# Storing the MLP's weight-block sums whole and splitting them where they are used

## The chip, the cores and the metric

The kernel runs on one core of a Trainium2 chip. A core has a matrix engine (PE, TensorE), a vector engine (DVE), a scalar engine (ACT), GpSimd (POOL) and a queue engine (SP) that here issues nearly all transfers (DMA). Matrix products write into PSUM, eight banks of 128 x 512 fp32; everything else lives in SBUF, 128 partitions wide. Each engine works off its own instruction stream in order and waits on semaphores for the others. The metric is device microseconds of one execution. The kernel before took 3085.63 us (median of 3 runs, 3080.34 to 3088.36).

## The reference, cut to what matters

One layer of a hybrid decoder runs on 2048 prompt tokens and 32 sample tokens (8 sequences of 4), all fp32, model width 1024:

```
h  = rmsnorm(x, g_mix);  proj = h @ w_in                 # 1024 x 4624
y  = [ RG-LRU mixer(proj) , Mamba-2 SSD mixer(proj) ]    # "the mixers"
x  = x + y @ w_out                                       # 2048 x 1024
m  = rmsnorm(x, g_mlp)
x  = x + square(relu(m @ w_up)) @ w_down                 # 1024 x 4096, 4096 x 1024
out = rmsnorm(x, g_final)
```

It also returns the states of both mixers. `w_up` and `w_down` are used by the MLP alone.

## The kernel before, in words

**Two-part products.** A matrix product of fp32 operands is made of three products of a reduced fp32 type (float32r). Each operand is split in a high part (ACT copies it to float32r) and a low part (DVE subtracts the high part from the original). The product adds high x high, high x low and low x high into one PSUM bank. `mm3` (lines 226 to 235) does so for the mixers, with weights split by `load_w` (an ACT copy in line 220, a DVE subtraction in line 222); `product` (lines 826 to 833) does it for the MLP.

**Mixers.** The 2080 tokens go through the mixers in three parts, each of two blocks of columns (384 and 384, 384 and 288, 384 and 256). In each part come the input projection and the SSD pairs (`pair_front`, `pair_x`, `pair_mats`, `pair_back`, eight times), then the LRU heads (`lru_front`, `lru_back`, eight times), then the output projection (`proj_add`, which multiplies and adds each PSUM bank on DVE, lines 445 and 446), then the transposes of the next part (`x_phase`).

**Weight blocks made in the mixers.** The MLP multiplies 2 x 2 blocks with seven products in place of eight (a Strassen-like scheme), so it needs seven combinations of each four weight blocks: four blocks and three sums. These don't depend on the tokens, and while the mixers run 64 jobs make them: 32 for `w_up`, 32 for `w_down`. A job has six stages: `job_load` issues eight DMAs of 64 KB into a tile `jt` of 128 x 7 x 256 (line 1128); `job_first` and `job_second` make the sums with four DVE additions of 128 x 256 (1133 to 1139); `job_higher` rounds all seven into a tile `jh` on ACT (1143); `job_lower` stores `jh` and starts to subtract, `job_store` subtracts the rest on DVE (1146) and stores the low parts (1150, 1155). `jt` and `jh` have one buffer each, so the next job's loads wait until both stores have landed. The mixers call `tick` at fixed places with a weight; each whole unit emits the next stage, 64 x 6 = 384 in all.

**MLP.** The tokens go through the MLP in three column blocks (2 x 348, 2 x 346, 2 x 346 columns). `front` loads the normalised tokens and makes the seven combinations of four k-blocks, each split in two. Then eight steps q follow: `up` twice (u = 0, 1), each seven products of 12 matmuls, with sums, relu, square and the seven combinations of the result (`operands`, `halves`) on ACT and DVE; then `down`, four groups g of seven products of 6 matmuls, each ended by a DVE addition out of PSUM (line 951). One weight load serves 12 matmuls: one product of `up`, or two of `down` (the seventh comes alone). The tile `mw` holds the high and the low parts and has six buffers; the DMA is issued by SP (lines 823 and 961). PSUM gives the products six banks, of which an `up` or a group of `down` takes four. In the last q of a column block the `front` of the next one is emitted among the groups of `down`, and the `final` norm of a block among the products of the next block's first two `up`s.

**What sets the order.** The framework orders each engine's instructions when the program is built: an instruction goes in when its inputs and buffers are planned to be there, earlier program text first. So the streams are not the program text; around the end of an `up`, PE takes the first halves of several `down` products before the second halves. Waits on the chip are fixed by that order.

## Time and profile before

| | before |
|---|---|
| median of 3 runs | 3085.63 us (3080.34 to 3088.36) |
| profiled execution | 3082.9 us, span 3081.2 us |
| PE busy | 2888.0 us (94%) |
| DVE busy | 2168.8 us (70%) |
| ACT busy | 1390.9 us (45%) |
| DMA | 708.99 MB, 230 GB/s; HBM read 541.43 MB, written 164.27 MB |
| mean granted TensorE clock | 0.970 |

The mixers take the time up to about 1700 us, the MLP the rest. A row of a windows view gives, for a stretch of the span, its length and then the busy microseconds of PE, PEld (the weight load of PE), DVE, ACT and POOL with the number of instructions, the granted TensorE clock, the DMA share and GB/s. A row of a group gives line, engine, operation, output <- input, shape and count, then busy time and mean duration, then the idle time of the engine before these and what ended it. A row of the chain of waits gives start, length and what the end of the program waited for at that time. A row of waits gives the waiting engine and line, what released it, the sum, the number of times and the longest.

### The profile page before, as it was taken

What the parts mean: (1) busy time and instruction counts of PE and PEld (TensorE: products, weight loads), DVE (VectorE), ACT (ScalarE), POOL (GpSimd) and SP (SyncE); (2) the same over time, 40 slices, a digit from 0 to 9 for tenths busy, and PEclk for the clock granted to TensorE, in tenths of its full rate; (3) what the DMA queues carried; (4) which work ended last, traced back from release to release, by engine and by line L of the source; (5) the groups of instructions that cost most, each with busy time, mean ns of one, the idle gap of its engine ahead of it and who ended that gap; (6) DMA issues with size and microseconds to landing.
All of it is one profiled execution on the core that took longest, in us unless ns stands there. A gap on an engine that the chain in (4) does not pass through costs nothing.

```text
span 3081.2 us, 49470 instructions
## 1 busy us (share of the span) xinstructions
PE 2888.0 (94%) x18150; PEld 2789.5 (91%) x18150; DVE 2168.8 (70%) x4422; ACT 1390.9 (45%) x2580; POOL 171.1 (6%) x270
## 2 busy tenths in 40 slices
PE   6999998989999898899989699999999999999997
PEld 6999897888988887899989599999999999999997
DVE  6888788688777878888787645556845556654556
ACT  5553685354357845444883323233432223432322
POOL 0000120010001300000120000000000000000000
PEclk9999998999999998999999799999999999999999
DMA  5555556766665577666656888888988888988885
GB/s 177 156 186 162 165 178 198 236 199 185 205 192 177 179 239 228 184 195 189 194 183 222 277 289 267 281 277 272 319 280 271 284 267 280 318 265 281 268 276 202
DMA packets 534481, 708.99 MB, mean 230 GB/s; under 512 B 44421, under 2 KB 414265, under 8 KB 534240
## 3 DMA queue, kind: packets, MB, share of 16 engines
q1 hardware_dynamic: 534016, 705.56, 71.8%
q8 instruction: 144, 2.36, 0.3%
q0 software_dynamic: 224, 0.27, 0.1%
q14 instruction: 97, 0.79, 0.1%
HBM read 541.43 MB, written 164.27 MB: 229 GB/s over the span
## 4 chain that ended last, share of the span: by engine, by line
PE 47%; DVE 8%; DMA 5%; ACT 4%; issue 1%; SPq 1%; POOL 0%; DVEq 0%; ACTq 0%
PE mb L832 39%; PE mm L235 2%; PE mm L233 2%; PE mm L234 2%; DVE jt L1146 1%; SPq L1128 1%; DMA dn<-jt 1%; DMA up<-jt 1%; DMA mb<-mn_d 1%; DMA mw<-dn 1%; DMA m<-cum 1%; DVE u L412 1%; DVE yt L1027 1%; DVE th L794 0%; ACT jh L1143 0%
## 5 line engine op out<-in xcount | busy, mean ns | idle before, releaser
L233 PE MATMUL mm<-xh,wh 128*128 128x384 f32 (+3 forms) x2160 | 712.6, 331 | 31.8 <-ACT xe L399 14.5
L235 PE MATMUL mm<-xh,wl 128*128 128x384 f32 (+3 forms) x2160 | 705.8, 328 | 3.9 <-DVE wl L222 3.8
L234 PE MATMUL mm<-xl,wh 128*128 128x384 f32 (+3 forms) x2160 | 705.4, 327 | 0.1
L832 PE MATMUL mb<-mhh,mw 128*128 128x346 f32 (+1 forms) x2688 | 655.2, 323 | 17.2 <-ACT mhh L839 16.6
L832 PE MATMUL mb<-ahh,mw 128*128 128x346 f32 (+1 forms) x2688 | 652.5, 323 | 13.1 <-DVE x L951 4.4
L832 PEld LDWEIGHTS mb<-mhh,mw 128*128 128x128 f32 x2688 | 475.8, 191 | 19.4 <-ACT mhh L839 18.3
L832 PEld LDWEIGHTS mb<-ahh,mw 128*128 128x128 f32 x2688 | 470.7, 189 | 19.6 <-ACT ahh L839 5.7
L233 PEld LDWEIGHTS mm<-xh,wh 128*128 128x128 f32 (+1 forms) x2160 | 409.0, 190 | 47.4 <-ACT xe L399 17.5
L832 PE MATMUL mb<-mhl,mw 128*128 128x346 f32 (+1 forms) x1344 | 437.3, 326 | 1.4 <-DVE mhl L840 1.4
L832 PE MATMUL mb<-ahl,mw 128*128 128x346 f32 (+1 forms) x1344 | 434.1, 323 | 0.4 <-DVE ahl L840 0.2
L235 PEld LDWEIGHTS mm<-xh,wl 128*128 128x128 f32 (+1 forms) x2160 | 408.2, 189 | 13.0 <-DVE wl L222 6.5
L234 PEld LDWEIGHTS mm<-xl,wh 128*128 128x128 f32 (+1 forms) x2160 | 409.0, 189 | 3.8 <-issue 1.0
L951 DVE TENSOR_TENSOR x<-x,mb 128x346 f32<-128x346 f32 (+1 forms) x480 | 244.5, 514 | 144.4 <-PE mb L832 143.1
L220 ACT ACTIVATE wh<-raw 128x1024 fp32r<-128x1024 f32 (+1 forms) x159 | 165.4, 1042 | 241.0 <-PE mm L234 181.0
L832 PEld LDWEIGHTS mb<-mhl,mw 128*128 128x128 f32 x1344 | 255.0, 190 | 2.8 <-DVE mhl L840 2.6
L832 PEld LDWEIGHTS mb<-ahl,mw 128*128 128x128 f32 x1344 | 253.7, 189 | 1.4 <-DVE ahl L840 1.4
L910 ACT ACTIVATE p<-mb 128x346 f32<-128x346 f32 (+1 forms) x48 | 21.9, 457 | 473.0 <-PE mb L832 470.9
L222 DVE TENSOR_TENSOR wl<-raw,wh 128x1024 fp32r<-128x1024 f32 (+1 forms) x159 | 190.7, 1201 | 20.5 <-ACT wh L220 19.4
L412 DVE SCALAR_TENSOR_TENSOR u<-xe,prm,u 128x768 f32<-128x768 f32 (+2 forms) x180 | 169.9, 944 | 16.6 <-ACT u L410 14.6
L233 PE MATMUL mm<-nh,wh 128*128 128x384 f32 (+2 forms) x384 | 131.2, 342 | 30.8 <-DVE x L446 27.8
L937 ACT ACTIVATE c<-c 128x346 f32<-128x346 f32 (+1 forms) x144 | 71.3, 495 | 192.5 <-DVE c L923 114.6
L1146 DVE TENSOR_TENSOR jt<-jt,jh 128x1024 fp32r<-128x1024 f32 (+1 forms) x128 | 137.9, 1094 | 25.0 <-ACT jh L1143 24.8
(305 smaller groups left out, 4218.6 us busy)
## 6 DMA issues: line engine op xcount, KB each, us to landing
mw<-up SPq DMA_DIRECT2D x336, 512.0 KB
mw<-dn SPq DMA_DIRECT2D x288, 512.0 KB
raw<-in_w_in_dram SPq DMA_DIRECT2D x108, 512.0 KB
up<-jh SPq DMA_DIRECT2D x32, 896.0 KB
up<-jt SPq DMA_DIRECT2D x32, 896.0 KB
dn<-jh SPq DMA_DIRECT2D x32, 896.0 KB
dn<-jt SPq DMA_DIRECT2D x32, 896.0 KB
raw<-in_w_out_dram SPq DMA_DIRECT2D x48, 512.0 KB
```

The source lines that it names most:

```text
L220: S.activation(h, raw, AF.Copy)
L222: V.tensor_tensor(out=lo, in0=raw, in1=h.bitcast(F32), op=ALU.subtract)
L233: T.matmul(ps[:m, :n], h[:, k, :m], xh[:, c0:c0 + n], start=k == 0, stop=False)
L234: T.matmul(ps[:m, :n], h[:, k, :m], xl[:, c0:c0 + n], start=False, stop=False)
L235: T.matmul(ps[:m, :n], lo[:, k, :m], xh[:, c0:c0 + n], start=False, stop=k == nk - 1)
L412: V.scalar_tensor_tensor(out=u[:, :W], in0=xe[:, k:k + W], scalar=pc(wn, k * nt + j), in1=u[:, :W], op0=ALU.mult, op1=ALU.add)
L832: T.matmul(ps[:, :n], w[:, wi, c], x[:, :n], start=start and k == 0 and i == 0, stop=k == nk - 1 and i == 2, skip_group_check=not start)
L937: S.activation(c[:, :n], c[:, :n], AF.Relu)
L951: V.tensor_tensor(out=c, in0=c, in1=ps[:, :n], op=op)
L1027: V.scalar_tensor_tensor(out=yt[:m], in0=src[:m], scalar=rs[:m, i:i + 1], in1=gfb[:m, 512 * hf:512 * hf + 512], op0=ALU.mult, op1=ALU.mult)
L1128: nc.sync.dma_start(t[:, at, 128 * k:128 * k + 128], dap(src, (r0 + dr_ * r + 128 * k) * ld + cols[i], [[ld, 128], [1, 128]]))
L1146: V.tensor_tensor(out=jt[j][:, a:b].bitcast(F32R), in0=jt[j][:, a:b], in1=jh[j][:, a:b].bitcast(F32), op=ALU.subtract)
```

## The change

- A job stores the seven combinations as they are, in fp32: its stages are `job_load`, `job_first`, `job_second` and the new `job_whole`, one store. `job_higher`, `job_lower` and `job_store` stay in the text but are selected by no job (the seventh entry of every job is False). `jt` gets two buffers. There are 64 x 4 = 256 stages, and `tick` is scaled by 256/384, so that a job spans the same ticks.
- The tensors in memory, `up_d` and `dn_d`, lose the axis of two: half the bytes.
- In the MLP a load brings the unsplit block into `mr` (128 x 512 fp32, NR = 4 buffers). `parts_of` splits it into `mw` (NM = 4 buffers) with one ACT copy and one DVE subtraction of 128 x 512 (128 x 256 for the single seventh `down` product). This happens for each of the three column blocks. `weights()` asks for loads up to NA = 3 ahead of the split and splits up to NP = 3 ahead of use. Before the first `front`, three loads are asked for and two tiles split, where five loads were issued.
- `mm3` does all products with the high part of the weights first, then all with the low part.

```diff
+UPJ, DNJ = True, True
+NR, NM, NA, NP = 4, 4, 3, 3
@@ mm3
             T.matmul(ps[:m, :n], h[:, k, :m], xh[:, c0:c0 + n], start=k == 0, stop=False)
             T.matmul(ps[:m, :n], h[:, k, :m], xl[:, c0:c0 + n], start=False, stop=False)
+
+        for k, (xh, xl) in enumerate(ops):
             T.matmul(ps[:m, :n], lo[:, k, :m], xh[:, c0:c0 + n], start=False, stop=k == nk - 1)
@@ mlp
-        def weights(src, op, m):
-            if src is up_d[0] and ahead:
-                return ahead.pop(0)
-            w = mp.tile([128, 2, 512], F32R, tag="mw", name="mw", bufs=6)
-            nc.sync.dma_start(w[:, :, :m].bitcast(F32), src[:, op])
+        def raw_weights(src, m):
+            t = mp.tile([128, 512], F32, tag="mr", name="mr", bufs=NR)
+            nc.sync.dma_start(t[:, :m], src)
+            return t
+
+        def parts_of(t, m):
+            w = mp.tile([128, 2, 512], F32R, tag="mw", name="mw", bufs=NM)
+            S.activation(w[:, 0, :m], t[:, :m], AF.Copy)
+            V.tensor_sub(w[:, 1, :m], t[:, :m], w[:, 0, :m].bitcast(F32))
             return w
...
+        def order():
+            for _ in MLP:
+                for q in range(NQ):
+                    for u in range(2):
+                        for op in range(7):
+                            yield ("u", up_d[2 * q + u], op)
+                    for g in range(4):
+                        for i in range(0, 7, 2):
+                            yield ("d", dn_d[4 * q + g], i)
...
+        def prepare():
+            if asked:
+                t, m = asked.pop(0)
+                ready.append(parts_of(t, m) if m else t)
+
+        def weights():
+            while len(asked) < NA:
+                n = len(asked)
+                ask()
+                if len(asked) == n:
+                    break
+            while len(ready) < NP and asked:
+                prepare()
+            return ready.pop(0)
@@ up, down
-            product(x, weights(src, 0, 512), mh[0], n, True)
+            product(x, upw(weights()), mh[0], n, True)
...
-                        t = mp.tile([128, 2, 512], F32R, tag="mw", name="mw", bufs=6)
...
+                        ws[0] = weights()
@@ end of mlp
-        ahead.extend([weights(up_d[0], op, 512) for op in range(5)])
+        while len(asked) < NA:
+            ask()
+        while len(ready) < NP - 1:
+            prepare()
@@ jobs
-    up_d = [dr.tile([128, 7, 2, 512], F32, name=f"up{j}") for j in range(2 * NQ)]
-    dn_d = [dr.tile([128, 7, 2, 256], F32, name=f"dn{j}") for j in range(4 * NQ)]
+    up_d = [dr.tile([128, 7, 512], F32, name=f"up{j}") for j in range(2 * NQ)]
+    dn_d = [dr.tile([128, 7, 256], F32, name=f"dn{j}") for j in range(4 * NQ)]
...
-        t = jt[j] = wp.tile([128, 7, 256], F32, tag="jt", name="jt", bufs=1)
+        t = jt[j] = wp.tile([128, 7, 256], F32, tag="jt", name="jt", bufs=2)
...
+    def job_whole(j):
+
+        nc.sync.dma_start(jobs[j][5], jt[j])
+        del jt[j]
...
-    stages = (job_load, job_first, job_second, job_higher, job_lower, job_store)
+    steps_ = [(st, j) for j in range(len(jobs)) for st in
+              (job_load, job_first, job_second) + ((job_higher, job_lower, job_store) if jobs[j][6] else (job_whole,))]
...
-        clock[1] += w * TF[clock[2]]
+        clock[1] += w * TF[clock[2]] * len(steps_) / 384
```

More of the change, by code (lines that the diff above doesn't have):

```diff
@@ new lines, in mlp, with ask @@
+        todo = order()
+        asked, ready = [], []
+        def ask():
+            e = next(todo, None)
+            if e is None:
+                return
+            kind, src, i = e
+            if kind == "u":
+                if UPJ:
+                    asked.append((raw_weights(src[:, i], 512), 512))
+                else:
+                    w, tv = whole_weights(src)
+                    nc.sync.dma_start(w.bitcast(F32), src[:, i])
+                    asked.append((w, 0))
+            else:
+                m = min(2, 7 - i)
+                if DNJ:
+                    asked.append((raw_weights(src[:, i:i + m].rearrange("p o c -> p (o c)"), 256 * m), 256 * m))
+                else:
+                    w, tv = whole_weights(src)
+                    nc.sync.dma_start(tv[:, :m * 512].bitcast(F32).rearrange("p (o c) -> p o c", c=512),
+                                      src[:, i:i + m].rearrange("p o h c -> p o (h c)"))
+                    asked.append((w, 0))
@@ L829, in product @@
             for k, (xh, xl) in enumerate(ops):
-                c = slice(128 * k, 128 * k + 128)
                 for i, (wi, x) in enumerate(((0, xh), (0, xl), (1, xh))):
-                    T.matmul(ps[:, :n], w[:, wi, c], x[:, :n], start=start and k == 0 and i == 0,
+                    T.matmul(ps[:, :n], w(wi, k), x[:, :n], start=start and k == 0 and i == 0,
                              stop=k == nk - 1 and i == 2, skip_group_check=not start)
@@ L910, in up @@
             S.activation(p1[:, :n], x[:, :n], AF.Copy)
-            product(y, weights(src, 1, 512), mh[1], n, True)
+            product(y, upw(weights()), mh[1], n, True)
             after(1, fill)
@@ L918, in up @@
             S.activation(p5[:, :n], z[:, :n], AF.Copy)
-            product(w, weights(src, 3, 512), mh[3], n, True)
+            product(w, upw(weights()), mh[3], n, True)
             after(3, fill)
@@ L1116, in hymba_step @@
                 jobs.append((w_up, FF, 256 * k, 512, [128 * (FQ * q + u + 2 * i) for i in range(2)],
-                             up_d[2 * q + u][:, :, :, 256 * k:256 * k + 256]))
+                             up_d[2 * q + u][:, :, 256 * k:256 * k + 256], False))
         for g in range(4):
-            jobs.append((w_down, D, 128 * FQ * q, 256, [128 * (g + 4 * i) for i in range(2)], dn_d[4 * q + g][:, :, :, :]))
+            jobs.append((w_down, D, 128 * FQ * q, 256, [128 * (g + 4 * i) for i in range(2)], dn_d[4 * q + g][:, :, :], False))
     jt, jh = {}, {}
@@ L1156, in job_store @@
         del jt[j], jh[j]
-    stages = (job_load, job_first, job_second, job_higher, job_lower, job_store)
+    steps_ = [(st, j) for j in range(len(jobs)) for st in
+              (job_load, job_first, job_second) + ((job_higher, job_lower, job_store) if jobs[j][6] else (job_whole,))]
     def tick(w):
-        n = len(stages)
-        clock[1] += w * TF[clock[2]]
-        while clock[1] >= 1 and clock[0] < n * len(jobs):
+        clock[1] += w * TF[clock[2]] * len(steps_) / 384
+        while clock[1] >= 1 and clock[0] < len(steps_):
             clock[1] -= 1
-            j, st = divmod(clock[0], n)
-            stages[st](j)
+            st, j = steps_[clock[0]]
+            st(j)
             clock[0] += 1
```

33 lines of the change are left out of this document (18 added, 15 removed).

## The prediction

> **What bounds the kernel now.** I read first the busy times, then windows by stage, then the chain of waits in the mixers, then one step q of the MLP in quarters.
>
> ```profile
> PE 2888.0 (94%) x18150; PEld 2789.5 (91%) x18150; DVE 2168.8 (70%) x4422; ACT 1390.9 (45%) x2580; POOL 171.1 (6%) x270
> ```
>
> ```profile
> 100.00:1700.00 1600.00, 1488.09 (x9479) 1411.91 (x9478) 1298.48 (x2423) 902.02 (x1455) 159.40 (x248) 0.96 0.63 193
> 1700.00:1740.00 40.00, 15.98 (x64) 13.32 (x64) 25.46 (x67) 10.47 (x25) 5.04 (x1) 0.58 0.78 273
> 1740.00:2142.20 402.20, 400.72 (x2506) 399.16 (x2506) 218.67 (x460) 124.56 (x284) 0.00 (x0) 1.00 0.86 280
> 2142.20:2209.20 67.00, 59.01 (x366) 55.79 (x366) 63.92 (x197) 38.54 (x99) 0.00 (x0) 0.99 0.85 284
> 2209.20:2590.00 380.80, 380.19 (x2385) 378.28 (x2384) 202.98 (x427) 108.80 (x245) 0.00 (x0) 1.00 0.86 284
> 2590.00:2657.00 67.00, 60.09 (x358) 56.67 (x358) 62.75 (x196) 37.58 (x95) 0.00 (x0) 0.95 0.84 281
> ```
>
> PE bounds the program, but not equally. In the mixers (first row) it idles 1600 - 1488 = 112 us, and the clock of 0.96 means 8% of the time at half rate, so up to 0.04 x 1600 = 64 us more. DVE is busy 81% there. Inside the MLP's column blocks (third and fifth row) PE is full and DVE only 54%. Between column blocks, where `front` and `final` run, DVE is busy 64 of 67 us and PE idles 8 and 7 us: there DVE is the bound already. A faster mixer is worth something only in its 112 + 64 us; a busier DVE costs at once between the column blocks.
>
> Where the mixers lose, the chain of waits shows the jobs:
>
> ```profile
> 1111.98 2.05 DVE jt L1146 x2
> 1114.06 6.51 DMA dn<-jt
> 1120.63 0.34 SPq L1128
> ...
> 1130.86 2.09 DVE jt L1146 x2
> 1132.98 5.91 DMA dn<-jt
> ```
>
> One job takes 1130.86 - 1111.98 = 18.9 us round its loop: subtract, land the store, issue eight loads, add, round. SP stands in line 1128 until the store has landed, and weight loads stand behind it.
>
> **The change part by part.** *The jobs.* The first two groups go; the third stays:
>
> ```profile
> L1146 DVE TENSOR_TENSOR jt<-jt,jh 128x1024 fp32r<-128x1024 f32 (+1 forms) x128 | 137.9, 1094 | 25.0 <-ACT jh L1143 24.8
> L1143 ACT ACTIVATE jh<-jt 128x1792 fp32r<-128x1792 f32 x64 | 108.6, 1697 | 98.8 <-DVE jt L1139 74.5 <-DMA raw<-in_w_out_dram 22.5 <-issue 1.4
> L1133 DVE TENSOR_TENSOR jt<-jt 128x256 f32<-128x256 f32 x64 | 27.4, 428 | 20.3 <-DMA jt<-in_w_up_dram 13.2 <-DMA jt<-in_w_down_dram 6.8
> ```
>
> That is 138 us of DVE and 109 of ACT, 64 of 128 stores, and, with two `jt`, the wait for the store. The 25 + 20 us that DVE idled for `jh` and `jt` go or shrink. PE gets back only what falls where it idles. Most of its idle time lies in eight stretches (300:360, 450:520, 590:670, 900:945, 1045:1110, 1150:1260, 1450:1480, 1570:1640), which sum to
>
> ```profile
> sum 530.00, PE 437.44 PEld 398.22 DVE 436.96 ACT 317.00 POOL 48.74; mean PE 54.68 PEld 49.78 DVE 54.62 ACT 39.62 POOL 6.09
> ```
>
> PE idles 93 of its 112 us there, with DVE at 82%. Jobs are spread evenly, so 530/1600 of the DVE work, 46 us, and of the idle 45 us, 15, leave these stretches. What PE waits for:
>
> ```profile
> PE mm L233 <- DVE x L446: 30.1, 14, 5.3
> PE mm L233 <- ACT xe L399: 14.5, 9, 3.8
> ...
> PE mm L235 <- DVE wl L222: 6.5, 8, 1.7
> ```
>
> PSUM banks that DVE empties late (L446) lead. I take two thirds of 46 + 15, since DVE's queue is what PE waits for most but not always: -41. Bounds: -8 (a sixth of the direct waits 30 + 14.5, about the share of the removed work) and -93 (all 61 and half of the clock's 64).
>
> *The order in `mm3`.* The low part of the weights is wanted 16 matmuls later (8 k, two each); a matmul of 384 columns follows the last after some 0.17 us (1488 us for 9479 of all shapes is 0.16), so 2.6 us, more than the longest of the waits for `wl`, 1.7: -6. The tokens' low operand is wanted sooner; no wait for it stands among the rows above, and I take 0, with the same 6 as the bound on that side.
>
> *The loads.*
>
> ```profile
> mw<-up SPq DMA_DIRECT2D x336, 512.0 KB
> mw<-dn SPq DMA_DIRECT2D x288, 512.0 KB
> ...
> mw<-dn SPq DMA_DIRECT2D x96, 256.0 KB
> ```
>
> All are halved. In the MLP the DMA share of 0.86 falls by nearly half, but PE waits little for it:
>
> ```profile
> PE mb L832 <- DVE x L951: 4.4, 2, 2.5
> PE mb L832 <- DMA mw<-dn: 4.3, 4, 1.9
> ```
>
> -4 (0 to -5).
>
> *The splits.* 624 of 128 x 512 and 96 of 128 x 256 come into the MLP, on ACT and DVE. No such size is there; I take spacing in a full queue from
>
> ```profile
> 1732.94 3.10 DVE L840 TENSOR_TENSOR mhl<-mb,mhh 128x348 fp32r<-128x348 f32 x7
> ```
>
> Seven of 348 columns take 3.10 us, 0.43 each with one tail of 0.51. Two of 1024 and 768 (mean 896) take 2.05, 1.03 each. The slope is 0.60/548 = 1.09 ns a column: 0.61 us for 512, 0.33 for 256, so 624 x 0.61 + 96 x 0.33 = 412 us of DVE. Bounds: 0.56 (the slope alone) and 0.68 (whole durations, between 0.51 at 348 and 1.094 at 896). ACT: 1697 ns for 1792 columns is 0.49 us for 512, some 330 us, and 490 if it took DVE's upper 0.68; with 125 of 402 us busy inside a block that brings it to two thirds at most, so it isn't the bound. 412 us on DVE against 138 removed: the gain must come from where they lie.
>
> [...]
>
> *A step q inside a column block*, in quarters of 13.4 us:
>
> ```profile
> 1834.00:1847.40 13.40, 13.40 (x86) 13.40 (x85) 4.15 (x9) 0.92 (x2) 0.00 (x0) 1.00 0.91 301
> 1847.40:1860.80 13.40, 13.40 (x86) 13.40 (x85) 7.38 (x17) 7.49 (x17) 0.00 (x0) 1.00 0.86 280
> 1860.80:1874.20 13.40, 13.40 (x85) 13.29 (x84) 9.31 (x21) 6.73 (x15) 0.00 (x0) 1.00 0.73 227
> 1874.20:1887.60 13.40, 13.40 (x87) 13.40 (x86) 7.81 (x16) 0.00 (x0) 0.00 (x0) 1.00 0.91 289
> ```
>
> A q has 14 + 12 wide and 4 narrow splits, 26 x 0.61 + 4 x 0.33 = 17.2 us, 4.3 a quarter: DVE comes to 8.5, 11.7, 13.6 and 12.1 of 13.4. On the mean (46 of 53.6) it fits; in the third quarter, where the second `up` ends and `down` begins, it doesn't. There DVE runs on without a pause:
>
> ```profile
> 1866.41 0.52 DVE L935 TENSOR_TENSOR c<-mb,v 128x348 f32<-128x348 f32 x1 [1.18 <-PE mb L832]
> ...
> 1872.96 0.93 DVE L951 TENSOR_TENSOR x<-x,mb 128x348 f32<-128x348 f32 x2
> 1874.28 0.52 DVE L951 TENSOR_TENSOR x<-x,mb 128x348 f32<-128x348 f32 x1 [0.40 <-PE mb L832]
> ```
>
> For 1873.9 - 1866.4 = 7.5 us it is late and only then waits for PE again. In that time PE uses 7.5/1.91 = 4 loads (12 matmuls each; 336 of them fill the 53.6 us, 0.16 each), whose splits add 4 x 0.57 = 2.3 us. The additions from PSUM come that much later, and PE's next products want those banks. Fillers are fewer too: with four `mw`, the next group's first load can't be split until this group's first is used up. PE can reorder around part of it: bounds 0 and 2.3 us; I take half, 1.15, at 22 of 24 joins (the other two lie in the next item): +25 (0 to 51).
>
> *Between column blocks.* DVE is full. PE's 59 us there are 31 loads, x 0.57 = 17.7 us more for DVE; at its 95% that stretches 67 by 18.5. The next quarter of PE's time has DVE slack of 13.4 - 7.2 - 4.3, about 2 us, to take over some (row 2209.20 below). +16.5 each, twice: +33 (20 to 42).
>
> *Start of the MLP.*
>
> ```profile
> 1713.89 2.50 SPq L823 DMA_DIRECT2D mw<-up  x5
> 1713.40:1726.80 13.40, 2.59 (x8) 2.33 (x9) 2.61 (x6) 1.91 (x4) 0.00 (x0) 0.50 0.99 352
> 1726.80:1740.20 13.40, 11.18 (x49) 9.23 (x47) 13.08 (x30) 7.89 (x20) 5.04 (x1) 0.75 0.91 310
> 2209.20:2222.60 13.40, 13.28 (x77) 12.99 (x77) 7.24 (x16) 0.92 (x2) 0.00 (x0) 0.92 1.02 389
> ```
>
> Five loads of 512 KB stand before the token loads at a DMA share of 0.99; three of 256 KB will: 1.8 MB less at 352 GB/s is -5 us. DVE then is full (13.08 of 13.4), and 49 matmuls are 4 loads: +2. Net -3 (-6 to +2).
>
> Sum: -41 - 6 - 4 + 25 + 33 - 3 = +4. The profiled execution took 3082.9 (span 3081.2), 2.7 below the median of the runs shown, so the median should come to 3085.6 + 4, about 3090. Mixers gain about 50 and the MLP gives it back.
>
> **The rivals.** *B, faster: the MLP swallows the splits and the mixers gain near their bound.* For it: PE's idle 112 + 64 us sit beside job work, and the job's loop blocks SP; the framework ordered PE around late inputs well enough to leave it full in every quarter. Against: DVE's third quarter. Price: mixers -61 - 6, half of the clock's loss that goes with those stalls -12, loads and start -7, joins +8, between blocks +33: -45, 3041.
>
> *C, slower: the joins stop the clock.* A stall of DVE's full lateness, 2.3 us at each join, may put PE to half rate for a spell. For it: after the first change of column block the window from 2209.20 has a clock of 0.92, so 16% of 13.4 us, 2.1 us, at half rate, and the second change 0.95 of 67 us, with no single wait of L832 for DVE over 2.5 us. Against: both came after a whole cluster of stalls, not after one. Price: 24 joins x (2.3 + 1.1, half of the 2.1 spent at half rate) = +82 in place of +25: 3090 + 57 = 3147. [...]
>
> [...]
>
> *D: nothing reaches PE on either side.* 3086, which lies inside the forecast.
>
> **How the numbers follow.** Forecast with D: 0.50, its own range 3064 to 3119 (half way to the bounds of the two largest unknowns: 26 down by the jobs; 16 up by the jobs and 13 by the joins). B 0.27, C 0.23. Runs tell a difference over 0.3%, 9 us, so no change is 3076 to 3095. Of the forecast's 0.50 some 0.13 lies below, 0.18 inside, 0.19 above. Faster 0.13 + 0.27 = 0.40; same 0.18; slower 0.19 + 0.23 = 0.42. The range reaches to B's and C's middle, since a tenth lies beyond each: 3030 to 3145.
>
> **What would show it.** Mixers: groups L1146 and L1143 gone, the MLP starting 40 to 55 us earlier than 1740, no line 1128 behind a store in the chain, waits for L446 under 25 us. MLP: a split at 0.55 to 0.65 us in the queue; DVE at 80 to 90% inside column blocks; the stretch between blocks 80 to 86 us; PE waits at each join for `x` or `u` of L951, `ahl` or `mw`, about 1 us. B is right if PE stays full in those quarters, C if the clock falls under 0.97 inside column blocks. The forecast is wrong if the MLP takes more than 90 us longer or the mixers gain under 20.

## The result and the profile after

The changed kernel takes 3040.76 us (median of 4 runs, 3038.79 to 3042.42), against 3086.84 for the kernel before on the same chip: a ratio of 0.9854, 95% interval 0.9837 to 0.9872. The forecast was 3090; the time is rival B's 3041.

The busy times of the changed kernel, and its window rows by stage. The first window ends where the last matmul of the mixers starts; the others end where the changed kernel has issued as many matmuls of the MLP as the kernel before had at the ends of its column blocks. Columns: length, then busy time of PE, PEld, DVE, ACT and POOL, granted clock, DMA share, GB/s.

```profile
PE 2894.0 (95%) x18150; PEld 2783.6 (92%) x18150; DVE 2447.2 (80%) x5014; ACT 1683.1 (55%) x3236; POOL 150.7 (5%) x270
```

```profile
100.00:1604.20 1504.20, 1455.78 (x9469) 1390.90 (x9469) 1176.95 (x2277) 803.07 (x1393) 141.75 (x248) 0.99 0.54 165
1651.80:2058.80 407.00, 405.87 (x2500) 398.45 (x2501) 340.85 (x680) 245.61 (x505) 0.00 (x0) 1.00 0.49 140
2058.80:2142.10 83.30, 67.44 (x367) 61.52 (x366) 78.76 (x224) 51.34 (x122) 0.00 (x0) 0.90 0.53 164
2163.60:2531.50 367.90, 364.69 (x2262) 358.78 (x2262) 306.97 (x613) 217.05 (x443) 0.00 (x0) 1.00 0.49 140
2531.50:2610.70 79.20, 65.83 (x360) 60.55 (x359) 72.95 (x213) 50.68 (x121) 0.00 (x0) 0.89 0.52 162
```

The same windows of the kernel before, cut at the same places of the work:

```profile
100.00:1694.20 1594.20, 1485.61 (x9460) 1409.86 (x9460) 1293.84 (x2408) 901.60 (x1454) 159.40 (x248) 0.96 0.63 193
1741.60:2142.50 400.90, 399.85 (x2503) 398.14 (x2501) 217.37 (x458) 124.30 (x282) 0.00 (x0) 1.00 0.85 280
2142.50:2209.20 66.70, 58.84 (x365) 55.76 (x366) 63.62 (x196) 38.24 (x98) 0.00 (x0) 0.99 0.85 284
2592.20:2657.00 64.80, 60.09 (x358) 56.67 (x358) 60.55 (x190) 37.58 (x95) 0.00 (x0) 0.95 0.83 281
```

The mixers end at 1604.2 in place of 1694.2: **-90.0 us**. In their window PE idles 1504.2 - 1455.8 = 48.4 us where it idled 1594.2 - 1485.6 = 108.6, so 60.2 of the 90 are idle time. The other 29.8 lie in busy time: 9469 matmuls are busy 1455.8 us, 9460 were 1485.6, at a granted clock of 0.99 in place of 0.96. The clock records of the two traces hold only full and half rate: in these windows PE was busy at half rate for 95 us before and for 43 after, which makes 26 of the 29.8.

The MLP, from that matmul to the end of the span, takes 3040.7 - 1604.2 = 1436.5 in place of 3081.2 - 1694.2 = 1387.0: **+49.5 us**. The stretches between the column blocks grew by 83.3 - 66.7 = 16.6 and by 79.2 - 64.8 = 14.4 us, 31 in all. The blocks grew by 407.0 - 400.9 = 6.1, by 5.7 (367.9 against 362.2, cut in the same way) and by 5.3 (385.3 against 380.0), 17 in all. The piece from the last matmul of the mixers to the first full block takes 47.6 against 47.4.

The chain that ended last, by engine and by line, of the kernel before and of the changed one:

```profile
PE 47%; DVE 8%; DMA 5%; ACT 4%; issue 1%; SPq 1%; POOL 0%; DVEq 0%; ACTq 0%
PE mb L832 39%; PE mm L235 2%; PE mm L233 2%; PE mm L234 2%; DVE jt L1146 1%; SPq L1128 1%; DMA dn<-jt 1%; DMA up<-jt 1%; DMA mb<-mn_d 1%; DMA mw<-dn 1%; DMA m<-cum 1%; DVE u L412 1%; DVE yt L1027 1%; DVE th L794 0%; ACT jh L1143 0%
```

```profile
PE 82%; DVE 9%; DMA 3%; ACT 3%; issue 2%; SPq 1%; DVEq 0%; ACTq 0%; POOL 0%
PE mb L894 40%; PE mm L236 11%; PE mm L240 11%; PE mm L237 11%; PE ax L723 1%; DMA m<-cum 1%; PE ax L719 1%; PE ax L695 1%; DMA xt<-in_x_prompt_dram 1%; DVE mw L830 1%; DVE mhl L902 1%; DVE yt L1090 1%; PE ax L635 1%; DVE u L417 1%; DVE th L799 0%
```

Before, the lines of a job (L1146, L1128, the stores from `jt`) stand on the chain and the three products of `mm3` have 2% each. After, no line of a job is among the first fifteen and the products have 11% each: the mixers are now bound mainly by their matmuls. A few pieces of jobs are left on the chain, the longest a load of `jt` of 4.61 us at 348.

The splits (groups; busy time, mean ns, then the idle time ahead of them and what ended it; each count of 720 is 624 wide and 96 narrow ones, so the means mix the two):

```profile
L829 ACT ACTIVATE mw<-mr 128x512 fp32r<-128x512 f32 x720 | 432.6, 602 | 442.5 <-PE mb L894 338.9
L830 DVE TENSOR_TENSOR mw<-mr,mw 128x512 fp32r<-128x512 f32 x720 | 468.7, 652 | 133.7 <-ACT mw L829 119.6
```

A stretch of DVE's queue, in order of time (start, length):

```profile
1904.78 0.42 DVE L830 TENSOR_TENSOR mw<-mr,mw 128x256 fp32r<-128x256 f32 x1
1905.11 0.51 DVE L1014 TENSOR_TENSOR u<-u,mb 128x348 f32<-128x348 f32 x1
...
1906.12 0.69 DVE L830 TENSOR_TENSOR mw<-mr,mw 128x512 fp32r<-128x512 f32 x1
1906.73 0.51 DVE L1014 TENSOR_TENSOR x<-x,mb 128x348 f32<-128x348 f32 x1
```

A wide split lasts 0.69 us, but the next operation starts 0.61 us after its start; a narrow one lasts 0.42 and takes 0.33 of the queue. These are the prediction's spacings to the hundredth; a price per split taken from the length would be 0.08 us too high in a full queue.

PE's waits in the MLP (what PE waited for: sum in us, times, longest):

```profile
PE mb L894 <- DVE u L1014: 11.3, 6, 3.4
PE mb L894 <- DVE x L1014: 8.9, 6, 3.0
...
PE mb L894 <- DVE mw L830: 4.9, 6, 1.5
PE mb L894 <- ACT mw L829: 3.1, 6, 1.8
```

and in the mixers, where line 451 is what line 446 was:

```profile
PE mm L236 <- DVE x L451: 12.2, 10, 2.5
PE mm L236 <- ACT xe L404: 6.8, 5, 2.3
```

In the mixers the wait for the output projection's additions, the prediction's L446, fell from 30.1 to 12.2 us. In the MLP the additions out of PSUM lead, 20 us in 12 waits, most of it between the column blocks; the tiles of the splits themselves are 8 us.

### The profile page after: what moved, and what is told of

The parts are those of the page before. It is cut to its first block, busy times and chain, and to the rows that moved or that the text cites. A ratio compares the mean times of both kernels' runs of the same rounds, so it can differ in the third digit from the quotient of the medians.

```text
span 3040.7 us, 51485 instructions
## 1 busy us (share of the span) xinstructions
PE 2894.0 (95%) x18150; PEld 2783.6 (92%) x18150; DVE 2447.2 (80%) x5014; ACT 1683.1 (55%) x3236; POOL 150.7 (5%) x270
## 4 chain that ended last, share of the span: by engine, by line
PE 82%; DVE 9%; DMA 3%; ACT 3%; issue 2%; SPq 1%; DVEq 0%; ACTq 0%; POOL 0%
PE mb L894 40%; PE mm L236 11%; PE mm L240 11%; PE mm L237 11%; PE ax L723 1%; DMA m<-cum 1%; PE ax L719 1%; PE ax L695 1%; DMA xt<-in_x_prompt_dram 1%; DVE mw L830 1%; DVE mhl L902 1%; DVE yt L1090 1%; PE ax L635 1%; DVE u L417 1%; DVE th L799 0%
## 5 line engine op out<-in xcount | busy, mean ns | idle before, releaser
L236 PE MATMUL mm<-xh,wh 128*128 128x384 f32 (+3 forms) x2160 | 687.6, 330 | 19.8 <-ACT xh L380 12.5
L894 PE MATMUL mb<-ahh,mw 128*128 128x346 f32 (+1 forms) x2688 | 671.0, 329 | 27.8 <-DVE u L1014 11.3
L237 PE MATMUL mm<-xl,wh 128*128 128x384 f32 (+3 forms) x2160 | 685.2, 329 | 1.3 <-DVE xl L381 1.1
L829 ACT ACTIVATE mw<-mr 128x512 fp32r<-128x512 f32 x720 | 432.6, 602 | 442.5 <-PE mb L894 338.9
L830 DVE TENSOR_TENSOR mw<-mr,mw 128x512 fp32r<-128x512 f32 x720 | 468.7, 652 | 133.7 <-ACT mw L829 119.6
L894 PEld LDWEIGHTS mb<-ahh,mw 128*128 128x128 f32 x2688 | 479.5, 192 | 48.3 <-DVE u L1014 13.2
L240 PE MATMUL mm<-xh,wl 128*128 128x384 f32 (+3 forms) x2160 | 395.2, 323 | 0.0
L240 PEld LDWEIGHTS mm<-xh,wl 128*128 128x128 f32 (+1 forms) x2160 | 349.5, 187 | 4.0 <-issue 0.5
L450 DVE TENSOR_TENSOR mm<-mm,bc 128x384 f32<-128x384 f32 (+2 forms) x144 | 75.0, 524 | 89.5 <-PE mm L240 88.3
L236 PE MATMUL mm<-nh,wh 128*128 128x384 f32 (+2 forms) x384 | 122.9, 329 | 13.0 <-DVE x L451 12.2
```

The costliest lines, as they stand in the source:

```text
L236: T.matmul(ps[:m, :n], h[:, k, :m], xh[:, c0:c0 + n], start=k == 0, stop=False)
L237: T.matmul(ps[:m, :n], h[:, k, :m], xl[:, c0:c0 + n], start=False, stop=False)
L240: T.matmul(ps[:m, :n], lo[:, k, :m], xh[:, c0:c0 + n], start=False, stop=k == nk - 1)
L450: V.tensor_mul(ps[:, :n], ps[:, :n], bc[:, c0:c0 + n])
L829: S.activation(w[:, 0, :m], t[:, :m], AF.Copy)
L830: V.tensor_sub(w[:, 1, :m], t[:, :m], w[:, 0, :m].bitcast(F32))
```

## The experiments

Two questions: which part of the job's work gave 90 us where 47 were reckoned, and whether the MLP's 49 come from DVE's load at the places that the prediction named. Each run is told by the time of the last matmul of the mixers ("mixers") and by what follows it to the end of the span ("MLP"). These two come from one profiled execution a run, while the executions of one kernel lie 3 to 19 us apart (e9: 2998.2 to 3016.7), so a few us in these columns say little.

| run | mixers | MLP | median us | ratio to before, 95% |
|---|---|---|---|---|
| before | 1694.2 | 1387.0 | 3080.8 to 3086.8 beside the others | |
| after | 1604.2 | 1436.5 | 3040.76 | 0.9837 to 0.9872 |
| e1 before, new `mm3` | 1683.8 | 1385.7 | 3072.82 | 0.9956 to 0.9982 |
| e2 after, old `mm3` | 1604.8 | 1435.5 | 3042.22 | 0.9861 to 0.9896 |
| e3 after, one `jt` | 1612.5 | 1432.8 | 3046.80 | 0.9869 to 0.9912 |
| e4 before, no split in jobs | 1639.0 | 1388.0 | 3026.71 | 0.9805 to 0.9844 |
| e5 after, each store twice | 1594.1 | 1433.9 | 3032.71 | 0.9814 to 0.9846 |
| e6 after, six stages a job | 1599.3 | 1434.5 | 3036.13 | 0.9824 to 0.9859 |
| e7 after, subtraction on GpSimd | 1603.4 | 1533.4 | 3128.64 | 1.0122 to 1.0156 |
| e8 after, five `mw`, two `mr` | 1601.6 | 1676.8 | 3280.97 | 1.0619 to 1.0654 |
| e9 e4 with two `jt` | 1615.6 | 1389.7 | 3006.75 | 0.9726 to 0.9778 |
| e10 e9 with new `mm3` | 1597.4 | 1386.5 | 2986.48 | 0.9669 to 0.9698 |
| e11 after, split in place, six `mw` | 1600.1 | 1438.3 | 3041.65 | 0.9849 to 0.9891 |
| e12 e11, low parts kept from block 1 | 1605.4 | 1461.5 | 3067.75 | 0.9936 to 0.9970 |
| e13 before, no subtraction in jobs | 1634.4 | 1386.2 | 3022.10 | 0.9792 to 0.9829 |
| e14 before, no rounding in jobs | 1686.9 | 1387.4 | 3076.95 | 0.9974 to 0.9996 |
| e15 e11, 8 jobs split in the mixers | 1597.9 | 1406.1 | 3006.15 | 0.9743 to 0.9782 |
| e16 e11, 15 jobs split in the mixers | 1601.6 | 1396.5 | 3001.00 | 0.9728 to 0.9762 |
| e17 e11, 22 jobs split in the mixers | 1606.6 | 1408.6 | 3017.56 | 0.9773 to 0.9812 |
| e18 e11, 29 jobs split in the mixers | 1621.3 | 1395.7 | 3022.76 | 0.9792 to 0.9824 |

### The mixers: the parts of the change one by one

**e1** puts the new order of `mm3` into the kernel before; **e2** takes it out of the changed one.

```diff
             T.matmul(ps[:m, :n], h[:, k, :m], xl[:, c0:c0 + n], start=False, stop=False)
+
+        for k, (xh, xl) in enumerate(ops):
             T.matmul(ps[:m, :n], lo[:, k, :m], xh[:, c0:c0 + n], start=False, stop=k == nk - 1)
```

> The kernel before with the new order in mm3 alone (all products with the high part of the weights first, then all with the low part). As the prediction priced it: 6 us less, 3081, the waits of PE for wl (6.5 us) gone and nothing else. Rival O (the order is worth much of the 92 us by which the mixers became shorter, because the subtraction for wl gets out of the way of DVE's other work): 25 us less or more, 3060, and the waits for L446 smaller too.

> The changed kernel with the old order in mm3. As the prediction priced it: 6 us more than the changed kernel, 3047. Rival O: 25 us more or above, 3066 or later, all of it in the mixers.

The order alone gains 10.4 us in the mixers (8.9 in the median); taken out of the changed kernel it costs 0.6. It is not the 25 us of rival O in either. That it costs nothing in the changed kernel isn't because DVE's queue has lost the jobs' subtractions: e10 below has lost them too, and there the order is worth 18.2.

**e3** gives `jt` one buffer again in the changed kernel.

```diff
-        t = jt[j] = wp.tile([128, 7, 256], F32, tag="jt", name="jt", bufs=2)
+        t = jt[j] = wp.tile([128, 7, 256], F32, tag="jt", name="jt", bufs=1)
```

> The changed kernel with one buffer for jt in place of two, so that a job's loads wait for the store of the job before, as before the change, but without the rounding and the subtraction in the loop. As the prediction priced it (the work on DVE counts, the wait for the store only through DVE's idle time): at most 10 us more, 3051. Rival S (the wait for the store, which blocks SP's queue, is the larger part): 30 to 50 us more, 3070 to 3090, with line 1128's successor back in the chain of waits.

It costs 8.3 us in the mixers, 6 in the median: within the prediction's 10 and far from rival S's 30 to 50.

**e4** leaves rounding and subtraction out of the jobs of the kernel before; the unsplit tile is stored twice, so that transfers and loads stay. The MLP then works with weights that are not split.

```diff
-        h = jh[j] = wp.tile([128, 7, 256], F32R, tag="jh", name="jh", bufs=1)
-        S.activation(h, jt[j], AF.Copy)
+        pass
...
-        nc.sync.dma_start(jobs[j][5][:, :, 0], jh[j].bitcast(F32))
-        lower(j, 0, 4)
+        nc.sync.dma_start(jobs[j][5][:, :, 0], jt[j])
...
-        lower(j, 4, 7)
```

**e9** adds the second `jt` to that, **e10** the new `mm3` to e9.

> The kernel before without the jobs' rounding on ACT and subtraction on DVE: jt is stored twice, at the same two stages, with one buffer; mm3 and the MLP are as before. It leaves out the split of the MLP's weights (both halves hold the unsplit block), so it prices the work alone. As the prediction priced it: 41 us less, 3046. Rival W (each us of DVE and ACT work in these stretches costs PE more than a us, by the clock too): 70 us less or more, 3016 or earlier. Rival S: 15 us less, 3072, because the loop with its store stays.

> The run without the job split (jt stored twice, old mm3, old MLP, six stages) with two buffers for jt. There the last product of the mixers ended at 1639, in the changed kernel at 1604, and neither the second store nor the pace of the stages explains it. If the wait for the store (one buffer, loads on the very next stage) is what is left, the last product comes at 1605 to 1615 and the time falls by about 27 us from 3027, to 3000. If the second buffer is worth only the 4 to 8 us that it is worth in the changed kernel, it stays at 3019 to 3023 and the new mm3 or the way the order falls must have the rest.

> The same with the new mm3: all of the change but the splits in the MLP (the weights are used unsplit in both halves, so the split is left out). The mixers should end as in the changed kernel, last product at 1604, and the MLP take what it took before, 1387 us after it against 1436 in the changed kernel: 2992. If the new mm3 does nothing here either, it equals the run with the old one within 9 us.

One after the other: the job's split -55.2 us, the second buffer -23.4, the new order -18.2, together -96.8. The split gives more than the 41 that the prediction had for the whole of the jobs and less than rival W's 70. The window rows of the mixers of e4, e9 and e10:

```profile
100.00:1639.00 1539.00, 1472.46 (x9462) 1403.53 (x9461) 1186.96 (x2284) 800.96 (x1392) 134.26 (x248) 0.97 0.66 200
```

```profile
100.00:1615.60 1515.60, 1461.92 (x9471) 1395.05 (x9470) 1181.16 (x2284) 801.79 (x1394) 144.52 (x248) 0.98 0.66 201
```

```profile
100.00:1597.40 1497.40, 1455.20 (x9472) 1389.84 (x9471) 1178.81 (x2284) 805.32 (x1394) 135.56 (x248) 0.99 0.67 204
```

PE's idle time goes from 108.6 over 66.5 and 53.7 to 42.2 us, and its busy time for the same matmuls from 1485.6 over 1472.5 and 1461.9 to 1455.2 while the granted clock climbs from 0.96 to 0.99. At every step the clock adds to what the shorter waits give. SP's wait for a job's stores is not what the split's 55 us are: between 100 and 1600 us line 1128 waits 97 us for the stores in the kernel before (50.6 and 46.4) and 161 in e4 (86.2 and 75.2). The shares depend on the order in which the parts are made (the `mm3` order is worth 18, 10 or 1 us, the buffer 23 or 8), so no single number belongs to one part.

**e5** stores each whole tile a second time, into a scratch tensor, so that a job has two stores as before; **e6** gives a job six stages, two of them empty, so that `tick` paces it as before.

```diff
+        nc.sync.dma_start(twin_d[j % 2][:, :, :], jt[j])
...
-              (job_load, job_first, job_second) + ((job_higher, job_lower, job_store) if jobs[j][6] else (job_whole,))]
+              (job_load, job_first, job_second, nothing, nothing, job_whole)]
```

> The changed kernel with a second store of each finished jt (896 KB to a scratch tensor that nothing reads), so that the jobs store as many bytes as before, but with neither rounding nor subtraction. It asks for the part of the mixers' 90 us that the work (55 us in the run without the job split) and the second jt (8 us) leave open. Theory B (bytes and SP's queue: the stores that went away gave it): the last product of the mixers at 1625 to 1635 in place of 1604, the time 20 to 30 us longer, 3065. Theory P (the pace of the stages gave it): at most 5 us longer.

> The changed kernel with six stages a job, two of them empty, so that the stages come at the places they had before: the additions one tick after the loads, in place of one and a half. Theory P: the last product of the mixers at 1625 to 1635, the time 20 to 30 us longer, and DVE's idle time before the first addition (line 1133 before) back to some 20 us. Theory B: at most 5 us longer.

Neither gives anything back; the mixers even end 10.1 and 4.9 us earlier. So neither the 64 stores nor the pace of the stages is a cause. These two also show how far an edit that removes no work can move the time: 5 to 8 us in the median, 5 to 10 in the mixers. Smaller steps than that, such as e3's 8 or e14's 7 below, can't be put down to one part.

**e13** leaves out the subtraction alone, **e14** the rounding alone; both keep both stores and one buffer.

```diff
-        V.tensor_tensor(out=jt[j][:, a:b].bitcast(F32R), in0=jt[j][:, a:b], in1=jh[j][:, a:b].bitcast(F32),
-                        op=ALU.subtract)
+        pass
```

```diff
-        h = jh[j] = wp.tile([128, 7, 256], F32R, tag="jh", name="jh", bufs=1)
-        S.activation(h, jt[j], AF.Copy)
+        pass
...
-        V.tensor_tensor(out=jt[j][:, a:b].bitcast(F32R), in0=jt[j][:, a:b], in1=jh[j][:, a:b].bitcast(F32),
+        V.tensor_tensor(out=jt[j][:, a:b].bitcast(F32R), in0=jt[j][:, a:b], in1=jt[j][:, a:b],
```

> The kernel before, with the jobs' subtraction on VectorE left out; the rounding on ScalarE and both stores stay, and the jobs' tiles have one buffer each. The low parts are not made, so the output is not the reference's. Leaving both steps out moved the last mixer product from 1694 to 1639, 55 us. If those 55 are VectorE's queue (the prediction's reasoning: 138 us of subtractions, 25 us of idle time for their input), this run has nearly all of them: last mixer product at 1640 to 1655, time 3028 to 3042. If they are ScalarE's rounding (109 us busy, priced at nothing by the prediction), it has few: 1675 to 1690, time 3065 to 3080. If it is the length of the job's loop, each gives its share of it: subtraction 2.1 of 3.8 us of work in the loop, some 30 us, last product near 1664, time 3052.

> The kernel before, with the jobs' rounding on ScalarE left out; VectorE subtracts a tile from itself instead, at the same size, and both stores stay. No split is made, so the output is not the reference's. If the 55 us are VectorE's queue: last mixer product at 1680 to 1692, time 3068 to 3083. If they are ScalarE's rounding: 1640 to 1655, time 3028 to 3042. If it is the length of the loop: rounding 1.7 of 3.8 us, some 25 us, near 1669, time 3057.

The window rows of the mixers, without the subtraction and without the rounding:

```profile
100.00:1634.40 1534.40, 1470.88 (x9462) 1404.74 (x9461) 1174.65 (x2279) 895.59 (x1451) 135.57 (x248) 0.97 0.65 199
```

```profile
100.00:1686.90 1586.90, 1486.20 (x9463) 1411.90 (x9462) 1297.03 (x2405) 802.11 (x1392) 158.42 (x248) 0.96 0.63 193
```

Without the subtraction DVE's busy time falls by 119 us and the mixers end 59.8 us earlier. Without the rounding ACT's falls by 99 and they end 7.3 earlier. So the whole of e4's 55 is DVE's subtraction; the length of the job's loop, which would have given the subtraction some 30 and the rounding some 25 by the expectations, is not the cause.

### The MLP: where the splits cost

**e10** above is the MLP without splits at use, with the same short mixers: 1386.5 us, the first block 400.0 us, and 66.6 and 65.3 between the blocks. The 49 us belong to what the change does in the MLP, and are not a consequence of the earlier start. Of that the runs below take the buffers (e11) and the splits' places (e15 to e18) apart.

**e7** moves the subtraction from DVE to GpSimd.

```diff
-            V.tensor_sub(w[:, 1, :m], t[:, :m], w[:, 0, :m].bitcast(F32))
+            G.tensor_tensor(out=w[:, 1, :m], in0=t[:, :m], in1=w[:, 0, :m].bitcast(F32), op=ALU.subtract)
```

> The changed kernel with the splits' subtraction on GpSimd, which is idle in the MLP. If DVE's load is what makes the MLP 50 us longer, as the prediction has it (joins 25, between column blocks 33), most of that goes: 35 to 50 us less than the changed kernel, 2990 to 3005. GpSimd's 128 x 768 took 1.54 us before, so a 128 x 512 some 1.05 us of the 1.91 that PE takes for a load: it should keep up. Rival N (ACT or the chain load, copy, subtract, product is what PE waits for): no gain, or slower than 3041.

The MLP takes 97 us more than in the changed kernel, where 35 to 50 less was expected. Groups of 1700 to 2000 us, first of this run (line 830 with its two shapes apart), then of the changed kernel:

```profile
L830 POOL TENSOR_TENSOR mw<-mr,mw 128x512 fp32r<-128x512 f32 x137 | 184.6, 1352 | 100.2 <-ACT mw L829 100.0
...
L902 DVE TENSOR_TENSOR ahl<-t,ahh 128x348 fp32r<-128x348 f32 x40 | 32.2, 833 | 2.6 <-ACT ahh L901 2.6
L902 DVE TENSOR_TENSOR ahl<-c,ahh 128x348 fp32r<-128x348 f32 x30 | 28.7, 968 | 12.2 <-ACT ahh L901 12.2
L1014 DVE TENSOR_TENSOR u<-u,mb 128x348 f32<-128x348 f32 x41 | 21.0, 512 | 11.4 <-PE mb L894 11.4
...
L911 DVE TENSOR_TENSOR t<-c,c 128x348 f32<-128x348 f32 x10 | 5.1, 508 | 0.0
```

```profile
L1014 DVE TENSOR_TENSOR u<-u,mb 128x348 f32<-128x348 f32 x40 | 20.4, 510 | 1.6 <-PE mb L894 1.6
L902 DVE TENSOR_TENSOR ahl<-c,ahh 128x348 fp32r<-128x348 f32 x34 | 17.6, 516 | 2.5 <-ACT ahh L901 1.9
```

A wide split takes GpSimd 1.35 us, against 0.61 of DVE's queue and the 1.05 of the expectation (its 1.54 us for 128 x 768 is a mean over three widths; 128 x 768 alone took 1.68 before), and it stands on the way to PE. In these 300 us, in which GpSimd is busy for 200, four groups of DVE's operations with both inputs in SBUF are longer: the two of line 902 take 833 and 968 ns in place of some 515, lines 909 and 910 take 698 and 1062 in place of 510 and 514. Three others with both inputs in SBUF are not: lines 987, 911 and 912 take 522, 508 and 507. The additions out of PSUM stay at 512. So the run frees DVE of the splits but slows much of what is left there, and says nothing on what DVE's load costs in the MLP.

**e8** trades two `mr` for a fifth `mw`, asks for loads two ahead of the split in place of three, and splits one product further ahead.

```diff
-NR, NM, NA, NP = 4, 4, 3, 3
+NR, NM, NA, NP = 2, 5, 2, 4
```

> The changed kernel with five mw and two mr in place of four and four (the same room), and splits up to four ahead. If PE waits at the joins because the fillers are gone (the next group's load can't be split), a product between 1700 and 2050 falls from 0.1617 us to about 0.160: 10 us less, 3031. If it is DVE's lateness, nothing changes, 3038 to 3044.

What ACT waited for from 1700 to 2000 us:

```profile
ACT mw L829 <- DMA mr<-dn: 69.2, 30, 4.3
ACT mw L829 <- DMA mr<-up: 38.3, 38, 3.3
```

With two `mr` the loads come late: ACT waits for them in 107 of 300 us, and the MLP grows by 240 us. The run says nothing on the number of `mw`; it shows that here loads two ahead come too late.

**e11** asks the same without that cost: the load goes into the first half of `mw` and is split in place, so there is no `mr` and there are six `mw`.

```diff
-NR, NM, NA, NP = 4, 4, 3, 3
+NR, NM, NA, NP = 4, 6, 3, 3
...
+            S.activation(t[:, 1, :m], t[:, 0, :m].bitcast(F32), AF.Copy)
+            V.tensor_sub(t[:, 0, :m], t[:, 0, :m].bitcast(F32), t[:, 1, :m].bitcast(F32))
```

> The changed kernel with the splits made in place: a load goes into the first half of mw, ACT rounds into the second half, DVE subtracts in place, so that all the room goes to six mw and no mr. Same work, same loads ahead. If PE's loss at the joins comes from the fillers that four mw don't allow, the products inside a column block fall from 0.1617 to about 0.159 us: 15 to 20 us less, 3021 to 3026. If it comes from DVE's lateness alone: within 9 us of 3041.

MLP 1438.3 against 1436.5: the shortage of buffers, the prediction's "fillers are fewer too", costs nothing here.

**e12** stores the low parts in the first block and loads them in the second and third in place of the subtraction.

```diff
+                    parts_of(w, m)
+                    nc.sync.dma_start(low, w[:, 0, :m].bitcast(F32))
...
+                nc.sync.dma_start(w[:, 1, :m].bitcast(F32), src)
+                nc.sync.dma_start(w[:, 0, :m].bitcast(F32), low)
```

> The same, but DVE subtracts only in the first column block, where each low part is also stored; the other two blocks load the block and its low part, and only ACT rounds. DVE's splits fall from 720 to 240. If DVE's load is what makes the MLP longer, two thirds of the 49 us go, all that the second change of block and the joins of blocks 2 and 3 cost: 3005 to 3010 (more with what the six buffers give). If the first block's stores, 63 MB on top of 63 MB of loads in some 430 us, hold it up, it stays at 3030 or above.

Windows, and what ACT waited for from 1650 to 2050 us:

```profile
1650.00:2050.00 400.00, 380.02 (x2290) 363.32 (x2288) 310.36 (x629) 217.93 (x454) 0.38 (x1) 1.00 0.80 257
2200.00:2500.00 300.00, 295.74 (x1846) 291.56 (x1845) 157.94 (x328) 174.69 (x366) 0.00 (x0) 1.00 0.82 269
```

```profile
ACT mw L828 <- DMA mw<-dn: 54.2, 48, 2.4
ACT mw L828 <- DMA mw<-up: 46.4, 33, 3.3
```

In the second block DVE is busy 53% of the time, against 83% in the changed kernel, but the DMA share is back at 0.8, ACT stands for the loads in the first block, and that block takes 436.4 us in place of 407.5. The second block is no shorter for DVE's smaller load, 371.3 us against 368.5 in e11; there, too, ACT waits for loads, 109.5 of 300 us. The time is 26 us worse than e11's, and the run doesn't part DVE's load from that of the transfers.

### Splits where DVE has room

**e15** takes e11 and leaves the splits of 8 jobs in the mixers: both `up` tensors of the first q and the `down` tensors of the last, which are the ones used between the column blocks. **e16** adds the first `down` group of every q (15 jobs).

```diff
+def split_up(q):
+    return q == 0
+
+
+def split_dn(q, g):
+    return q == FF // 128 // FQ - 1
...
-            jobs.append((w_down, D, 128 * FQ * q, 256, [128 * (g + 4 * i) for i in range(2)], dn_d[4 * q + g][:, :, :], False))
+            jobs.append((w_down, D, 128 * FQ * q, 256, [128 * (g + 4 * i) for i in range(2)], (dn_d[4 * q + g], slice(0, 256)), split_dn(q, g)))
```

> The changed kernel with the splits in place (six buffers, as in the run before this set that took 3041.7), and with the weights that are used between the column blocks split in the mixers as before: 8 of 64 jobs (up of the first step q, down of the last), loaded in two parts. If the 33 us between the blocks are VectorE's load of splits there, the two stretches go back to some 15 us lost each from 30, the MLP takes 1404 to 1410 instead of 1438 after the last mixer product, and the mixers lose at most 8/64 of 55, some 7 us: time 3010 to 3025. If instead the stretches are long for another reason (the later start of the first loads, the order there), the MLP stays above 1430 and the time is 3040 to 3050.

> The same with the first group of the down weights of every step q split in the mixers too: 15 of 64 jobs. These are the weights used at the joins from up to down. If the joins' cost is VectorE's lateness there, as predicted, their 16 us shrink to some 8, against some 6 more in the mixers: MLP 1394 to 1402, time 3005 to 3022, about the same as with 8 jobs. If the joins' cost doesn't hang on the splits at that place: MLP as with 8 jobs, time 5 to 10 above that run.

Windows of e15, the two stretches between the blocks, and of e16, the mixers and the first stretch:

```profile
2050.50:2117.20 66.70, 59.47 (x367) 56.60 (x366) 63.88 (x197) 38.73 (x98) 0.00 (x0) 0.97 0.88 293
2508.60:2573.50 64.90, 59.28 (x359) 56.02 (x359) 61.08 (x191) 39.61 (x101) 0.00 (x0) 0.97 0.85 286
```

```profile
100.00:1601.60 1501.60, 1458.48 (x9475) 1394.74 (x9474) 1206.25 (x2313) 824.05 (x1407) 139.17 (x248) 0.98 0.57 175
...
2053.10:2118.70 65.60, 58.25 (x367) 55.31 (x366) 62.64 (x195) 36.76 (x95) 0.00 (x0) 1.00 0.88 292
```

With 8 jobs the stretches are back at 66.7 and 64.9 us, the 66.7 and 64.8 of before, and the MLP loses 32 of e11's 1438: what was lost between the blocks were the splits there, where DVE was busy 78.8 of 83.3 and 73.0 of 79.2 us. The mixers pay nothing that could be told for 8 or 15 of 64 splits. **e16 beats both kernels**: 3001.0 us, ratio 0.9745 to the kernel before. But not for the reason that it was made for: its first and third block take 405.5 and 384.9 us against 406.0 and 385.3 in e15 (the second 365.1 against 369.4), so most of the joins' loss stayed.

**e17** and **e18** look for that loss ahead of the join: the second `up` of every q split in the mixers as well, added to e15 (22 jobs) and to e16 (29 jobs).

```diff
-def split_up(q):
-    return q == 0
+def split_up(j):
+    return j == 0 or j % 2 == 1
```

> The kernel of the run with 8 jobs split in the mixers, and the second up group of every step q split there too: 22 of 64 jobs. If VectorE's lateness at the joins comes from the splits of the second up group, ahead of the join, the five late products go: blocks of 400 to 402 and 380 to 382 us instead of 406.0 and 385.3, MLP 1389 to 1394 after the last mixer product. The mixers split 14 jobs more; 8 and 15 jobs cost them nothing that could be told, 64 cost 60, so 0 to 12 here: time 2992 to 3010. If the lateness has another source, the blocks stay and the time is 3004 to 3018.

> Both the second up group and the first down group of every step q, the first up group and the last step's down groups split in the mixers: 29 of 64 jobs. If the splits ahead of the join are the source, the blocks are those of the run with 22 jobs (400 to 402, 380 to 382) and the mixers lose up to 7 more: time 2992 to 3015, no better than with 22. If both groups together make it, only this run has blocks under 402.

Neither theory holds: the first block takes 411.3 and 405.7 us, the third 386.7 and 386.1. The joins' loss hangs neither on the splits ahead of the join nor on those behind it alone. And the mixers now pay: 5 us at 22 jobs (against 15), 20 at 29. So there is room on DVE in the mixers for some 15 jobs, and not for 29.

What the trace of the changed kernel shows at a join, in order of time (DVE's two steps for `t`, ACT's rounding, PE's weight loads that wait; in brackets the idle time before and what ended it):

```profile
1780.50 0.51 DVE L909 TENSOR_TENSOR t<-c,c 128x348 f32<-128x348 f32 x1
...
1780.93 0.42 DVE L830 TENSOR_TENSOR mw<-mr,mw 128x256 fp32r<-128x256 f32 x1
...
1781.27 0.51 DVE L910 TENSOR_TENSOR t<-c,t 128x348 f32<-128x348 f32 x1
...
1781.81 1.26 ACT L901 ACTIVATE ahh<-t 128x348 fp32r<-128x348 f32 x3 [0.17 <-DVE t L910]
...
1782.36 0.19 PEld L894 LDWEIGHTS mb<-ahh,mw 128*128 128x128 f32 x1 [0.24 <-ACT ahh L901]
...
1782.74 0.19 PEld L894 LDWEIGHTS mb<-ahh,mw 128*128 128x128 f32 x1 [0.20 <-ACT ahh L901]
...
1783.13 0.19 PEld L894 LDWEIGHTS mb<-ahl,mw 128*128 128x128 f32 x1 [0.20 <-DVE ahl L902]
```

PE doesn't wait for the additions out of PSUM here but for the combined activations of `down`, which DVE adds, ACT rounds and DVE subtracts one piece after another; here a narrow split stands 0.34 us between the two additions. Five matmuls are late, by some 0.7 us in all, and the same ones at every join inside a block. With that split gone (e16) the delays change from join to join. At one of its longest, ACT's queue and PE's weight load that waits for it:

```profile
2785.55 0.63 ACT L830 ACTIVATE mw<-mw 128x512 fp32r<-128x512 f32 x1 [1.28 <-DMA mw<-dn]
2786.09 0.47 ACT L988 ACTIVATE c<-c 128x346 f32<-128x346 f32 x1
2786.47 0.48 ACT L886 ACTIVATE ahh<-t 128x346 fp32r<-128x346 f32 x1
...
2787.00 0.45 PEld L879 LDWEIGHTS mb<-ahh,mw 128*128 128x128 f32 x3 [1.38 <-ACT ahh L886]
```

Here the rounding of a weight tile that is still split in the MLP (line 830) stands in ACT's queue ahead of the activations' square and rounding (lines 988 and 886). ACT waits 1.28 us for that tile's load, and PE is 1.38 us late. A join of e18 (2193.4) has the same with 0.64 us of waiting for the load. In e15 (2171.2) and e17 (1783.8) PE waits 1.0 us for the activations' low part, which stands on DVE behind a weight's subtraction that waits for ACT's rounding. So taking some splits away lets others stand in the chain; without any (e10) the blocks are as short as before. That all joins are late for this reason is argued from these places, not shown.

## Why the prediction was wrong

**The failing step is the term for the jobs, -41** ("I take two thirds of 46 + 15"), and with it the decision to leave the clock's 64 us out of the sum. The reason behind it was right: e13 shows that DVE's queue is what the mixers waited for, and e14, with 7 us, that ACT's 109 us were rightly priced at next to nothing. The size was off. In the order of e4, e9 and e10, the split and the second buffer gave 55 + 23 = 78 in place of 41: 55 of it in idle time of PE and 24 in busy time at the higher clock.

- *What PE gets back where it idles.* The idle time fell by 60.2 us. The step had 61 to give and took two thirds of it, and with the 6 of `mm3` came to 47. Two thirds had no row behind it: through e4 and e9 PE's idle time went from 108.6 to 53.7 us, 55 of the 61.
- *The clock.* 29.8 us, half of the 64 that the first window row of before shows as lost to half rate. The prediction saw the number, put half of it into the bound of -93 and nothing into the centre. In every one of e4, e9, e10 and e13 the clock is higher (0.97 to 0.99) where PE's idle time is less. The bound was "all 61 and half of the clock's 64"; the mixers moved by 60 and 30.
- *`mm3`, -6.* 10.4 alone, 18.2 as the last step of e10, 0.6 when undone in the changed kernel.
- *Loads and the start, -4 and -3.* The start came to +0.2; of the loads nothing could be told apart.
- *Splits, 0.61 and 0.33 us.* Right, as the queue's rows show. ACT came to 246 of 407 us in the first block, 60%, within "two thirds at most", and DVE to 84%.
- *Joins, +25.* 17 us, 0.7 a join. The size was near, the mechanism was not: not the banks, in the rows at the join, nor the fillers (e11), but the chain that makes `ahh` and `ahl`. Splits in the queues of DVE and ACT stand in that chain at the places shown; how the 17 us divide over all joins stays open.
- *Between the blocks, +33.* 31 us (16.6 and 14.4), and e15 shows the splits there to be the reason, as the step had it. Part of it came by a way that the step did not have: the granted clock there fell to 0.90 and 0.89, from 0.99 and 0.95.
- *A sum beside the forecast.* The bound of -8 takes a sixth for the share of the removed work, but 138 of DVE's 1298 us is about a ninth. It doesn't move the forecast.

The sum was +4; with -90 for -47 in the mixers and +49.5 for +51 in the rest it is -40.5, the change of the span from 3081.2 to 3040.7.

**Rival B** gave 3041 from -79 in the mixers, -7 for loads and start, and +41 behind them; measured were -90, nothing, and +49. Its two thoughts, a gain near the bound and a share of the clock (it took 12 of 30), are what happened; its price for the joins, 8, was as far off as the forecast's 25. That its total came to the measured time within 1 us is luck: its three pieces miss by 11, 7 and 8 us and nearly cancel. "PE stays full in those quarters", by which it was to be known, is not quite so.

**Rival C** put half-rate spells at the joins. Inside the blocks the clock is 1.00 with those 0.7 us lost at each join, so it fell. Half-rate spells did come between the blocks, where the waits stand in clusters, the longest 3.4 us in the row for `u` above: the granted clock was 0.90 over the 83.3 us of the first stretch and 0.89 over the 79.2 of the second. From what length of wait on the clock falls was not shown.

**Rival D** is ruled out by the interval.

## What to carry to other kernels

Where the bounding engine's waits end on one queue, as here, expect most of what leaves that queue in those stretches to come back (55 of 61 us), and price the spells at half clock that go with the waits (95 us of PE's busy time in the mixers before, 43 after). Work moved from a stage with slack to another should be moved piece by piece: here the splits used where DVE is full stay cheap in the stage before (15 of 64 jobs cost nothing there), and the others cost less where they are used (17 us at 24 joins) than in the mixers (e13: 60 for all 64). Gains of several edits to the same stage don't add (the order of `mm3` gave 10, 18 or 1 us), so each is measured alone and as the last one.

## What the runs showed of the hardware

- DVE slowed beside GpSimd in e7: two groups of operations with both inputs in SBUF went from some 515 ns to 833 and 968 on the mean, a factor of 1.6 to 1.9, while GpSimd subtracted tiles of 128 x 512 at 1.35 us each; those with an input in PSUM stayed at 512, and three groups with both inputs in SBUF stayed at 507 to 522.
- The length of a DVE operation and what it takes of a full queue differ: 0.69 and 0.61 us for 512 columns, 0.42 and 0.33 for 256 (rows at 1904.78 and 1906.12 of the changed kernel).
- A third of the gain in the mixers, 30 of 90 us, is less busy time for the same matmuls at a higher granted clock (0.96 to 0.99). The clock rises from run to run as PE's idle time falls: 108.6 us at 0.96, 66.5 at 0.97, 53.7 at 0.98, 48.4 and 42.2 at 0.99.
